# Attention in a decoder trunk on one core: the softmax steps drawn together, two residual tiles loaded a block sooner, and the maximum's tile in a pool of its own

## The chip, the cores and the metric

One core of a Trainium2 chip runs the whole program. The metric is the device time of one execution in microseconds (us). The kernel before has a median of 2106.7 us over three runs (2106.67 to 2110.82).

## What is computed

Two layers over a sequence of 1024 tokens of width 1024, all in fp32: a gated short convolution and then dilated attention, each followed by a SwiGLU network. The change touches the attention alone. Cut to that part, the reference is

```python
BRANCHES = ((128, 1), (512, 4), (2048, 16))          # window, dilation; 16 heads of 64

def dilated_attention_mixer(h, w_qkv, w_out, rel_bias):
    qkv = (h @ w_qkv).reshape(bsz, seq, 3, N_HEADS, HEAD_DIM)
    q, k, v = qkv[:, :, 0], qkv[:, :, 1], qkv[:, :, 2]
    for window, dilation in BRANCHES:
        o, l = dilated_branch(q, k, v, rel_bias, window, dilation)   # banded, causal, biased
        outs.append(o); lses.append(l)
    alpha = jax.nn.softmax(jnp.stack(lses, axis=0), axis=0)
    o = jnp.sum(alpha[..., None] * jnp.stack(outs, axis=0), axis=0)
    return o.reshape(bsz, seq, D_MODEL).astype(h.dtype) @ w_out      # added to x
```

Weighting the branches by their log-denominators is the same as one softmax over the keys of all three, and that is how the kernel computes it: for each head one maximum, one set of exponentials and one sum.

## The kernel before, in words

Every product is split: an operand becomes a rounded high part and a remainder, and three matmuls (high by high, high by low, low by high) stand for one. The two dense networks use Strassen-like schemes; they surround the attention and are not touched. The five engines each work through an instruction list of their own in order; the order in which the program's text issues the work is the order on each engine, and semaphores alone join them.

`attention` handles the 16 heads in 17 calls of `slot`, called **blocks 0 to 16** here. Block `n` holds the scores of head `n`, the softmax of head `n-1`, and the product with the values (called pv) of head `n-1`, and fills the rest of TensorE's time with dense work: up to block 10 the value projection (`value_tiles`), from block 11 on the first half of the output projection (`out_product`), whose results are added to the residual tiles `X`. A block has two halves. In the first, a loop of eight rounds takes one softmax step of the former head, one score step of this head and some dense matmuls in each round; in the second, the pv matmuls run with more dense work.

A score step gives one PSUM bank, which VectorE (DVE) empties with the bias added: into `lf` (two steps), `lh`, then `ld` and `lp` (four steps, called j0, j2, j4 and j6). Between them DVE builds the running maximum `m`: after `lh` its second half begins, after j2 its first half is complete, after j6 the second. GpSimd (POOL) then takes the maximum over the partitions of each half (`partition_all_reduce`, tile `mb`). There are eight PSUM banks, handed out in rotation.

A softmax step is a subtraction of `mb` on DVE and an exponential on ScalarE (ACT) of the same tile. There are seven: first-half `lf`, `ld`, `lp`, then second-half `lf`, `lh`, `ld`, `lp`. The pv matmuls read them in this order: first half `lf`, `ld`, `lp`; second half `lf`, `lh`, `ld`, `lp`. From block 14 on (`n > LAG`) the order is another: the softmax of a head runs whole, inside the block of its scores, and the table of this change is not read there (block 13 still reads it for head 12).

ACT also makes `kca`, a copy of the next head's keys sorted by residue, in two pieces (`classes`, in the second half of a block); the next block's first score matmuls read it.

All large tiles share one pool of 41 pages of 512 KB (`page`), used in rotation: a new tile waits until the last reader of the page's former tile is done. SyncE (SP) issues nearly all loads, in order, and an issue that waits holds up those behind it. In a block it issues the keys (`ka`), in even blocks the values (`vx`), then the queries (`qa`, `ql`) and the bias of the next head, then `oin` in blocks 9 and 10 (finished heads, read back from DRAM), then what the dense work asks for: raw weights, and in `out_product` the residual tiles `X[k]` from `spill[k]`, three tiles ahead of the one that is added to.

Of the kernel before, what the change touches and what calls it, by code (L numbers as in the profile page):

```python
# [10 lines left out]
F32 = mybir.dt.float32  # L11
# [6 lines left out]
S = 1024  # L18
# [30 lines left out]
AO_WIDE = 5  # L49
AO = 4  # L50
LAG = 13
EXTRA = (3, 7)
FILL = (("v", 0), ("v", 1), ("v", 2), ("v", 3))
OIN = LAG - 3
DENSE = (11,) * 9 + (10, 10) + (11, 11, 14, 10, 10, 9)
# [47 lines left out]
def trunk(ctx: ExitStack, tc: tile.TileContext, x, gains_in, cwi, ck, cwo, wqkv, wo, relb,  # L103
          wg, wu, wd, oneh, ident, out):
    nc = tc.nc
# [6 lines left out]
    def page(name, dt=F32):  # L112
        return pages.tile([128, 1024], dt, name=name, tag="page", bufs=PAGES)

    scope = {}
# [4 lines left out]
    def bank():  # L120
        return psum.tile([128, 512], F32, name="bank", tag="bank")
# [288 lines left out]
    X = [None] * KT  # L410
# [140 lines left out]
    class Strassen:  # L551
# [216 lines left out]
        def load_x(self, *ns):  # L768
            for n in ns:
                X[n] = page("x")  # L770
                nc.sync.dma_start(X[n], self.source[n])
# [651 lines left out]
    spill = [dram.tile([128, 1024], F32, name=f"spill{n}") for n in range(KT)]  # L1423
# [70 lines left out]
    def attention(norm, qk):  # L1494
# [57 lines left out]
        def load_kq(n):  # L1552
# [7 lines left out]
            nc.sync.dma_start(KS[n][n1].bitcast(F32), rows(k, 128 + 64 * a))  # L1560
            if n <= LAG + 1 and n % 2 == 0 and n:
                load_values(p - 1)
# [11 lines left out]
        def scores(p, a, st):  # L1574

            n = 2 * p + a
            ks, kc, qs = KS[n], KC[n], QS[n]
            q2 = qlo[a]
            bias = st["bias"]
            lf, lh, ld, lp = page("lf"), half_page("lh"), page("ld"), page("lp")  # L1580
            st.update(lf=lf, lh=lh, ld=ld, lp=lp)

            klass = lambda u: kc[:, u * 128:u * 128 + 128]
            block = lambda u: ks[:, u * 128:u * 128 + 128]

            def mm(o, k, qoff, qdims):
                nc.tensor.matmul(o, k, view(qs, qoff, qdims), start=True, stop=False)  # L1587
                nc.tensor.matmul(o, k, view(q2, qoff, qdims), start=False, stop=True)  # L1588

            kd = [[128, 4], [1, 32]]  # L1590

            for c in range(2):
                b = bank()
                for i in range(2):
                    r4 = 2 * c + i
                    mm(b[:, 256 * i:256 * i + 256], klass(r4), r4 * 32, [[512, 2], [128, 4], [1, 32]])
                for ih in range(2):
                    nc.vector.tensor_tensor(out=view(lf, ih * HALF + 64 * c, [[128, 4], [32, 2], [1, 32]]),
                                            in0=view(b, 128 * ih, [[32, 4], [256, 2], [1, 32]]),
                                            in1=view(bias, L1 + L2 - 1 - 32 * ih, [[-A2, 4], [0, 2], [-1, 32]]),  # L1600
                                            op=ALU.add)
                yield

            b = bank()
            for r4 in range(4):
                mm(b[:, 128 * r4:128 * r4 + 128], klass(4 + r4), HALF + r4 * 32, kd)
            nc.vector.tensor_tensor(out=view(lh, 0, [[128, 4], [32, 4], [1, 32]]),
                                    in0=view(b, 0, [[32, 4], [128, 4], [1, 32]]),
                                    in1=view(bias, L1 + L2 - 1, [[-A2, 4], [0, 4], [-1, 32]]), op=ALU.add)
            m = page("m")  # L1610
            st["m"] = m
            nc.vector.tensor_tensor(out=m[:, HALF:], in0=lf[:, HALF:], in1=lh, op=ALU.max)
            yield

            for j in range(0, 8, 2):
                b = bank()
                for i in range(2):
                    jj = j + i
                    if jj < 7:
                        mm(b[:, 256 * i:256 * i + 256], block(jj),  # L1620
                           blk(jj), [[blk(jj + 1) - blk(jj), 2], [32, 16], [1, 8]])
                    else:
                        mm(b[:, 256:384], block(jj), blk(jj), [[32, 16], [1, 8]])
                nc.vector.tensor_tensor(out=view(ld, blk(j), [[32, 16], [8, 2], [1, 8]]),
                                        in0=view(b, 0, [[8, 16], [256, 2], [1, 8]]),
                                        in1=view(bias, L1 - 1, [[-A1, 16], [0, 2], [-1, 8]]), op=ALU.add)
                n = 2 if j < 6 else 1
                step = blk(j + 2) - blk(j + 1) if n == 2 else 8
                nc.vector.tensor_tensor(out=view(lp, blk(j + 1), [[32, 16], [step, n], [1, 8]]),
                                        in0=view(b, 128, [[8, 16], [256, n], [1, 8]]),  # L1630
                                        in1=view(bias, L1 - 1 - 8, [[-A1, 16], [0, n], [-1, 8]]), op=ALU.add)
                if j == 2:
                    nc.vector.tensor_tensor(out=m[:, :HALF], in0=lf[:, :HALF], in1=ld[:, :HALF], op=ALU.max)
                    q = lambda t: view(t, 8, [[32, 16], [1, 24]])
                    nc.vector.tensor_tensor(out=q(m), in0=q(m), in1=q(lp), op=ALU.max)
                    mb = page("mb")
                    st["mb"] = mb
                    nc.gpsimd.partition_all_reduce(mb[:, :HALF], m[:, :HALF], 128, bass_isa.ReduceOp.max)
                yield
            nc.vector.tensor_tensor(out=m[:, HALF:], in0=m[:, HALF:], in1=ld[:, HALF:], op=ALU.max)  # L1640
            nc.vector.tensor_tensor(out=m[:, HALF:], in0=m[:, HALF:], in1=lp[:, HALF:], op=ALU.max)
            nc.gpsimd.partition_all_reduce(mb[:, HALF:], m[:, HALF:], 128, bass_isa.ReduceOp.max)
            yield
# [84 lines left out]
        put_off, ending, due = [], [], [iter(())]  # L1728
        OZ, acts = {}, {}

        def slot(n, dense, ndense, late=0, hook=iter(()), ps=()):
# [12 lines left out]
            if n + 1 < H:  # L1744
                load_kq(n + 1)
                bias[n + 1] = load_bias(n + 1)
            done.update(load_attended(ps))
            if n:
                q, b = divmod(n - 1, 2)
                if b == 0:  # L1750
                    OZ[q] = page("o"), page("z")
                old = live.pop(n - 1)
                old.update(o=OZ[q][0], z=OZ[q][1])
                pv = values(q, b, old)
            else:
                pv = iter(())
            extra = later = iter(())
            lagged = n <= LAG
            if n + 1 < H:
# [3 lines left out]
            used = 0  # L1763
            if lagged:
                for i in range(8):
                    next(due[0], None)
                    next(sc, None)
                    k = 1 + (i in EXTRA and n < LAG) if n else i % 2
                    other(k)
                    used += k  # L1770
                    if a and ending and i == 4:
                        run(ending.pop())
                run(sc)
            else:
                if a == 0 and not late:
                    other(1)
                    used += 1
                for i in range(8):
                    next(sc, None)
                    next(pv, None)  # L1780
                    next(pv, None)
                    if i >= late and i % 2 == 0:
                        other(1)
                        used += 1
                run(sc)
                run(pv)
                if a == 0:
                    extra = finish(p - 1)
                if a == 0 and n < H:
                    load_values(p)  # L1790
            left = max(ndense - used, 0)
            for i in range(8):
                next(pv, None)
                next(pv, None)
                if i == (2 if n > LAG + 1 else 5):
                    attended()
# [12 lines left out]
            run(pv)  # L1809
            run(extra)  # L1810

        def load_attended(ps):
            raw = {p: page("oin") for p in ps}
            for p in ps:
                nc.sync.dma_start(raw[p], odram[p])
            return raw
# [6 lines left out]
        def out_product(g, ps, acts):  # L1823
            for n in range(KT):
                w = take(("ao", g, n))
                for k in range(n, min(n + 3, KT)):
                    if X[k] is None:
                        X[k] = page("x")
                        nc.sync.dma_start(X[k], spill[k])
                for c in HALVES:  # L1830
                    b = bank()
                    yield from product(w, ps, acts, {c: b})
                    add_to_x(n, {c: b})
# [97 lines left out]
        sw.feed_forward(*rest, after)  # L1931
        qk.mix()
    with tc.tile_pool(name="second", bufs=1) as scope["pool"]:
        scope["halves"] = 8
        acts = attention(norm, qk)
    with tc.tile_pool(name="third", bufs=1) as scope["pool"]:
        scope["halves"] = 20
# [118 lines left out]
```

## Time and profile before

| | |
|---|---|
| median of three runs | 2106.7 us (2106.67 to 2110.82) |
| the profiled execution | 2106.85 us, of which 2105.1 us from the first to the last instruction |
| TensorE, DVE, ACT, POOL busy | 99%, 84%, 48%, 12% of the span |
| attention, blocks 0 to 15 | about 1143 to 1411 us of the span |
| scores of head 10 begin (block 10) | 1297.28 us |
| scores of head 11 begin (block 11) | 1313.27 us |
| scores of head 12 begin (block 12) | 1334.74 us |

A row of the timeline gives the start from the span's begin, the duration, the engine, the line, the operation, what is written and read, and in brackets how long the engine had been idle and what ended that. Consecutive like instructions are merged (x8). Matmul ends are modelled, and a row of matmuls may run into the next, so the rate of TensorE is read from the starts. An fp32 matmul of pv is recorded as two. A row of the stretches (windows) gives the busy time of each engine, the granted TensorE clock as a share of full speed, and the mean busy share of the 16 DMA engines.

### The profile page before, as it was taken

To read this page: it belongs to the slowest core of one execution; us is meant where nothing else is said; L and a number is where in the kernel's file an instruction comes from. 1 tells how busy PE (TensorE), PEld (TensorE's weight loads), DVE (VectorE), ACT (ScalarE), POOL (GpSimd) and SP (SyncE) were. 2 spreads that over 40 slices of the span, in tenths; PEclk is the share of its full clock that TensorE was granted. 3 is DMA by queue.
4 is the path that set the end of the run, shared out by engine and by line. 5 is a ranking of instruction groups with operands and counts; after the bars stand their busy time and mean duration, and the time that the engine had idled before them with its cause. 6 is when DMAs were issued, how large, how long until landed. Compare 5 with 4: busy or idle time off the path is not lost.

```text
span 2105.1 us, 30800 instructions
## 1 busy us (share of the span) xinstructions
PE 2080.8 (99%) x10978; PEld 1790.0 (85%) x10978; DVE 1760.2 (84%) x3308; ACT 1020.9 (48%) x1892; POOL 250.1 (12%) x352
## 2 busy tenths in 40 slices
PE   9999999999999999999999999999999999999998
PEld 7888888888888888887789999898788888888887
DVE  8898769988888888968975888887998888888886
ACT  7433427443434554445543666565644434456433
POOL 1000000110101010010323333211011001001000
PEclk9999999999999999999999999999999999999999
DMA  7322643223333466341757767855223333358432
GB/s 220 95 95 71 230 136 75 106 101 110 113 102 106 152 205 205 125 158 68 235 175 219 193 177 202 237 179 157 71 86 107 108 99 113 110 193 245 159 95 81
DMA packets 124729, 300.72 MB, mean 143 GB/s; under 512 B 15084, under 2 KB 37694, under 8 KB 124576
## 3 DMA queue, kind: packets, MB, share of 16 engines
q1 hardware_dynamic: 90720, 201.94, 31.6%
q0 software_dynamic: 26224, 82.11, 12.5%
q10 hardware_dynamic: 7632, 14.70, 1.9%
q8 instruction: 87, 1.43, 0.3%
q14 instruction: 66, 0.54, 0.1%
HBM read 208.42 MB, written 82.93 MB: 138 GB/s over the span
## 4 chain that ended last, share of the span: by engine, by line
PE 48%; DVE 4%; ACT 1%; DMA 1%; issue 0%; DVEq 0%; ACTq 0%
PE bank L587 9%; PE bank L585 9%; PE bank L586 9%; PE bank L1662 4%; PE bank L387 2%; PE bank L389 2%; PE bank L388 2%; PE bank L1531 1%; PE bank L677 1%; PE bank L1533 1%; PE bank L1532 1%; PE bank L680 1%; PE bank L679 1%; PE bank L1588 1%; PE bank L1587 1%; DVE w L147 1%
## 5 line engine op out<-in xcount | busy, mean ns | idle before, releaser
L587 PE MATMUL bank<-b,w 128*128 128x512 f32 x2008 | 782.6, 390 | 4.8 <-DVE w L147 4.5
L585 PE MATMUL bank<-b,w 128*128 128x512 f32 x2008 | 782.7, 390 | 4.4 <-ACT w L146 2.2
L586 PE MATMUL bank<-b,w 128*128 128x512 f32 x2008 | 782.1, 390 | 0.6 <-DVE b L896 0.6
L587 PEld LDWEIGHTS bank<-b,w 128*128 128x128 f32 x2008 | 376.9, 188 | 88.1 <-DVE w L147 9.9
L585 PEld LDWEIGHTS bank<-b,w 128*128 128x128 f32 x2008 | 377.2, 188 | 82.7 <-ACT w L146 3.3
L586 PEld LDWEIGHTS bank<-b,w 128*128 128x128 f32 x2008 | 377.2, 188 | 78.1 <-DVE b L896 1.2
L146 ACT ACTIVATE w<-combo 128x512 fp32r<-128x512 f32 (+2 forms) x496 | 253.9, 542 | 239.2 <-DVE combo L207 220.4
L147 DVE TENSOR_TENSOR w<-combo,w 128x512 fp32r<-128x512 f32 (+2 forms) x496 | 282.6, 583 | 37.8 <-ACT w L146 37.0
L591 ACT ACTIVATE part<-bank 128x512 f32<-128x512 f32 x192 | 114.2, 595 | 381.0 <-PE bank L587 379.1
L147 DVE TENSOR_TENSOR w<-raw,w 128x512 fp32r<-128x512 f32 (+2 forms) x348 | 193.1, 576 | 38.9 <-ACT w L146 38.9
L595 DVE TENSOR_TENSOR part<-part,bank 128x256 f32<-128x256 f32 (+1 forms) x372 | 175.2, 501 | 32.0 <-PE bank L587 17.4
L146 ACT ACTIVATE w<-raw 128x512 fp32r<-128x512 f32 (+2 forms) x348 | 170.5, 531 | 56.1 <-PE bank L587 21.5
L387 PE MATMUL bank<-w_hi,w 128*128 128x512 f32 (+1 forms) x400 | 151.8, 380 | 0.1
L389 PE MATMUL bank<-w_hi,w 128*128 128x512 f32 (+1 forms) x400 | 149.5, 374 | 0.7 <-DVE w L147 0.7
L388 PE MATMUL bank<-w_lo,w 128*128 128x512 f32 (+1 forms) x400 | 149.3, 373 | 0.0
L506 DVE TENSOR_TENSOR x<-x,bank 128x512 f32<-128x512 f32 (+1 forms) x104 | 66.6, 644 | 63.4 <-PE bank L389 58.2
L815 DVE TENSOR_TENSOR x<-x,bank 128x512 f32<-128x512 f32 x136 | 92.9, 683 | 28.6 <-PE bank L587 28.6
L207 DVE TENSOR_TENSOR combo<-raw 128x512 f32<-128x512 f32 (+1 forms) x176 | 114.0, 649 | 0.0
L389 PEld LDWEIGHTS bank<-w_hi,w 128*128 128x128 f32 x400 | 75.5, 189 | 15.1 <-DVE w L147 1.6
L578 DVE TENSOR_TENSOR b<-hin,b 128x512 fp32r<-128x512 f32 x126 | 79.6, 686 | 9.3 <-ACT b L577 9.2
L387 PEld LDWEIGHTS bank<-w_hi,w 128*128 128x128 f32 x400 | 75.7, 189 | 11.9 <-ACT w L146 0.5
L388 PEld LDWEIGHTS bank<-w_lo,w 128*128 128x128 f32 x400 | 75.8, 189 | 11.6
(228 smaller groups left out, 3352.1 us busy)
## 6 DMA issues: line engine op xcount, KB each, us to landing
hin<-part SPq DMA_DIRECT2D x126, 256.0 KB, 5.0
raw<-in_ffn_w_gate SPq DMA_DIRECT2D x44, 512.0 KB
raw<-in_ffn_w_up SPq DMA_DIRECT2D x44, 512.0 KB, 3.7
part<-sum POOLq DMA_DIRECT2D x72, 256.0 KB, 2.3
raw<-in_ffn_w_down SPq DMA_DIRECT2D x48, 384.0 KB, 3.2
raw<-in_attn_w_qkv SPq DMA_DIRECT2D x27, 512.0 KB, 5.3
raw<-in_conv_w_in SPq DMA_DIRECT2D x24, 512.0 KB, 3.6
part<-part POOLq DMA_DIRECT2D x36, 256.0 KB, 2.5
```

The costliest lines, as they stand in the source:

```text
L146: nc.scalar.activation(hi, src, AF.Copy)
L147: low = lambda: eng.tensor_tensor(out=lo, in0=src, in1=hi, op=ALU.subtract)
L207: eng.tensor_tensor(out=c, in0=a, in1=b, op=op)
L387: nc.tensor.matmul(b, whi[:, a], ahi[:, s], start=first, stop=False)
L388: nc.tensor.matmul(b, whi[:, a], alo[:, s], start=False, stop=False)
L389: nc.tensor.matmul(b, wlo[:, a], ahi[:, s], start=False, stop=last)
L585: nc.tensor.matmul(b, hi[:, a], bhi, start=start and k == 0, stop=False, skip_group_check=True)
L586: nc.tensor.matmul(b, hi[:, a], blo, start=False, stop=False, skip_group_check=True)
L587: nc.tensor.matmul(b, lo[:, a], bhi, start=False, stop=k == n - 1, skip_group_check=True)
L591: nc.scalar.activation(t, b, AF.Copy)
L595: nc.vector.tensor_tensor(out=t, in0=t, in1=b, op=ALU.add)
L815: nc.vector.tensor_tensor(out=X[n][:, half(h)], in0=X[n][:, half(h)], in1=b, op=ALU.add)
```

## The change

Four edits.

1. A table `PIECES` says how many softmax steps each of the eight rounds takes: 1, 1, 2, 2, 1 and then none, where it was one in each of the first seven.
2. At the start of block 10 (`n == OIN`), behind the loads of `oin`, the residual tiles `X[0]` and `X[1]` are loaded. `out_product` no longer finds them missing in block 11 and loads `X[2]` there.
3. The tile `m` comes from a pool of two buffers of its own, tagged `max`, and no longer from the 41 pages.
4. The pool of half pages in the attention has 4 buffers and not 8, which is the room that the two buffers of `m` take.

```diff
+PIECES = (1, 1, 2, 2, 1) + (0,) * 3
...
-            m = page("m")
+            m = scope["pool"].tile([128, S], F32, name="m", tag="max", bufs=2)
...
             done.update(load_attended(ps))
+            if n == OIN:
+                for k in range(2):
+                    load_x(k)
...
             if lagged:
                 for i in range(8):
-                    next(due[0], None)
+                    for _ in range(PIECES[i]):
+                        next(due[0], None)
                     next(sc, None)
...
+        def load_x(k):
+            if X[k] is None:
+                X[k] = page("x")
+                nc.sync.dma_start(X[k], spill[k])
...
                 for k in range(n, min(n + 3, KT)):
-                    if X[k] is None:
-                        X[k] = page("x")
-                        nc.sync.dma_start(X[k], spill[k])
+                    load_x(k)
...
     with tc.tile_pool(name="second", bufs=1) as scope["pool"]:
-        scope["halves"] = 8
+        scope["halves"] = 4
```

TensorE's list is the same, instruction for instruction. In the changed kernel line numbers are higher by one from here on, and by more behind `load_x`.

DVE in block 11, from the `lh` score step to the second residual add. A row whose source and target is `mb` and one of `lf`, `lh`, `ld`, `lp` is a softmax subtraction, `x<-x,bank` is the residual add. Before:

```order
L1607 TENSOR_TENSOR lh<-bank,bias 128x512
L1612 TENSOR_TENSOR m<-lf,lh 128x512
L1651 TENSOR_TENSOR lf<-lf,mb 128x512
L1624 TENSOR_TENSOR ld<-bank,bias 128x16x16
L1629 TENSOR_TENSOR lp<-bank,bias 128x16x16
L1651 TENSOR_TENSOR lh<-lh,mb 128x512
L1624 TENSOR_TENSOR ld<-bank,bias 128x16x16
L1629 TENSOR_TENSOR lp<-bank,bias 128x16x2x8
L1633 TENSOR_TENSOR m<-lf,ld 128x512
L1635 TENSOR_TENSOR m<-m,lp 128x16x24
L506 TENSOR_TENSOR x<-x,bank 128x512
L1651 TENSOR_TENSOR ld<-ld,mb 128x512
```

The same place on DVE after the change, from the same `lh` score step on; the row just ahead of it is now `lf<-lf,mb`:

```order
L1608 TENSOR_TENSOR lh<-bank,bias 128x512
L1613 TENSOR_TENSOR m<-lf,lh 128x512
L1652 TENSOR_TENSOR lh<-lh,mb 128x512
L1652 TENSOR_TENSOR ld<-ld,mb 128x512
L1625 TENSOR_TENSOR ld<-bank,bias 128x16x16
L1630 TENSOR_TENSOR lp<-bank,bias 128x16x16
L1652 TENSOR_TENSOR lp<-lp,mb 128x512
L1625 TENSOR_TENSOR ld<-bank,bias 128x16x16
L1630 TENSOR_TENSOR lp<-bank,bias 128x16x2x8
L1634 TENSOR_TENSOR m<-lf,ld 128x512
L1636 TENSOR_TENSOR m<-m,lp 128x16x24
L507 TENSOR_TENSOR x<-x,bank 128x512
```

The four second-half subtractions moved up: `lf` ahead of the `lh` score step, `lh` and `ld` ahead of j0, `lp` ahead of j2. All stand ahead of the residual add now, where `ld` and `lp` stood behind it. The same move is made in blocks 1 to 13.

SP at the end of the loads of block 10, into block 11 (`odram` holds finished heads, `kq` keys and queries, `vdram` values). Before:

```order
L1815 DMA oin<-odram_88 128x1024
L170 DMA raw<-in_attn_w_out 128x512
L1559 DMA ka<-kq_1_2926 64x1024
L1560 DMA ka<-kq_1_2926 64x1024
L1546 DMA vx<-vdram_95 128x8x128
L1549 DMA vx<-vdram_95 128x4x128 x2
L1564 DMA qa<-kq_0_2925 64x1024 x2
L1565 DMA ql_10353<-kq_0_2925 64x1024
L1482 DMA bias<-tables 128x1x361
L1483 DMA bias<-tables 128x1x349
L1829 DMA x<-spill_77 128x1024
L1829 DMA x<-spill_78 128x1024
```

The same place on SP after the change:

```order
L1825 DMA oin<-odram_88 128x1024
L1820 DMA x<-spill_77 128x1024
L1820 DMA x<-spill_78 128x1024
L171 DMA raw<-in_attn_w_out 128x512
L1560 DMA ka<-kq_1_2926 64x1024
L1561 DMA ka<-kq_1_2926 64x1024
L1547 DMA vx<-vdram_95 128x8x128
L1550 DMA vx<-vdram_95 128x4x128 x2
L1565 DMA qa<-kq_0_2925 64x1024 x2
```

The two residual loads moved past eleven issues: one of raw weights, two of keys, three of values, three of queries and two of the bias.

## Prediction, before the run

> **What bounds the kernel now.** I read the page's busy shares first, then the waits of TensorE over the attention (1130 to 1500 us), then the timelines of the engines that those waits name, then 4-us stretches around them.
>
> ```profile
> span 2105.1 us, 30800 instructions
> PE 2080.8 (99%) x10978; PEld 1790.0 (85%) x10978; DVE 1760.2 (84%) x3308; ACT 1020.9 (48%) x1892; POOL 250.1 (12%) x352
> ...
> PE bank L1662 <- ACT ld L1652: 2.0, 1, 2.0
> PE bank L1662 <- ACT lp L1652: 1.0, 2, 0.8
> ```
>
> TensorE is busy for 2080.8 of 2105.1 us and its instruction list does not change. So the change can only give back time in which TensorE stands idle or runs at a lower clock, at most 24.3 us plus what the clock costs, and it can only lose time by making TensorE wait where it does not wait now. In the waits, pv (L1662) waits three times for an exponential: once for `ld`, 2.0 us, and twice for `lp`, 1.0 us. Where these are, TensorE's timeline shows (blocks 6, 9, 10 and 11, the ends of pv and the starts of the next scores):
>
> ```profile
> 1246.43 0.39 PE L1662 MATMUL bank<-ld,vx 128*128 128x128 f32 x2
> 1247.08 0.49 PE L1662 MATMUL bank<-lp,vx 128*128 128x128 f32 x2 [0.27 <-ACT lp L1652]
> ...
> 1297.13 0.39 PE L1662 MATMUL bank<-lp,vx 128*128 128x128 f32 x2
> 1297.28 0.37 PE L1587 MATMUL bank<-qa,kca 128*128 128x256 f32 x1
> ...
> 1310.15 1.06 PE L1662 MATMUL bank<-lh,vx 128*128 128x128 f32 x8
> 1311.04 0.39 PE L1662 MATMUL bank<-ld,vx 128*128 128x128 f32 x2
> 1311.28 0.49 PE L1662 MATMUL bank<-lp,vx 128*128 128x128 f32 x2
> ...
> 1312.72 0.39 PE L1662 MATMUL bank<-lp,vx 128*128 128x128 f32 x2
> 1313.27 0.38 PE L1587 MATMUL bank<-qa,kca 128*128 128x256 f32 x1 [0.16 <-ACT kca L1571]
> ...
> 1323.71 1.05 PE L1662 MATMUL bank<-lf,vx 128*128 128x128 f32 x8
> 1327.06 1.06 PE L1662 MATMUL bank<-lh,vx 128*128 128x128 f32 x8
> 1330.11 0.49 PE L1662 MATMUL bank<-ld,vx 128*128 128x128 f32 x2 [2.00 <-ACT ld L1652]
> 1331.38 0.49 PE L1662 MATMUL bank<-lp,vx 128*128 128x128 f32 x2 [0.78 <-ACT lp L1652]
> ```
>
> The two large waits are both in block 11. DVE's timeline, block 10 above and block 11 below, says why:
>
> ```profile
> 1306.58 0.42 DVE L1624 TENSOR_TENSOR ld<-bank,bias 128x256 f32<-128x256 f32 x1
> 1307.24 0.68 DVE L1633 TENSOR_TENSOR m<-lf,ld 128x512 f32<-128x512 f32 x1
> 1308.44 0.68 DVE L1651 TENSOR_TENSOR ld<-ld,mb 128x512 f32<-128x512 f32 x1
> 1309.04 0.42 DVE L1624 TENSOR_TENSOR ld<-bank,bias 128x256 f32<-128x256 f32 x1
> 1309.71 0.86 DVE L1651 TENSOR_TENSOR lp<-lp,mb 128x512 f32<-128x512 f32 x1
> ...
> 1318.72 0.68 DVE L1607 TENSOR_TENSOR lh<-bank,bias 128x512 f32<-128x512 f32 x1
> 1320.06 0.68 DVE L1651 TENSOR_TENSOR lf<-lf,mb 128x512 f32<-128x512 f32 x1
> 1320.66 0.42 DVE L1624 TENSOR_TENSOR ld<-bank,bias 128x256 f32<-128x256 f32 x1
> 1323.30 0.56 DVE L1635 TENSOR_TENSOR m<-m,lp 128x384 f32<-128x384 f32 x1
> 1328.10 0.69 DVE L506 TENSOR_TENSOR x<-x,bank 128x512 f32<-128x512 f32 x1 [4.25 <-DMA x<-spill]
> 1328.71 0.68 DVE L1651 TENSOR_TENSOR ld<-ld,mb 128x512 f32<-128x512 f32 x1
> ```
>
> In block 11 DVE reaches the first residual add, finds `X[0]` not landed, and stands for 4.25 us. The second half's `ld` and `lp` subtractions are queued behind that add. Their exponentials follow, and pv behind those. In block 10, without a residual add, the same `ld` subtraction runs at 1308.44.
>
> ```profile
> 1310.60 0.63 ACT L1652 ACTIVATE lp<-lp 128x512 f32<-128x512 f32 x1 [0.81 <-DVE lp L1651]
> 1312.08 1.13 ACT L1571 ACTIVATE kca<-ka 128x512 fp32r<-128x512 f32 x1
> ...
> 1308.00:1312.00 4.00, 4.00 (x37) 3.96 (x36) 3.96 (x9) 2.03 (x3) 2.14 (x1) 1.00 0.87 257
> 1312.00:1316.00 4.00, 3.80 (x28) 3.12 (x27) 2.97 (x6) 3.96 (x6) 2.15 (x1) 1.00 0.39 104
> 1332.00:1336.00 4.00, 4.00 (x19) 3.64 (x19) 4.00 (x6) 3.95 (x6) 2.35 (x2) 0.57 1.02 224
> ...
> 1298.35 7.64 SPq L1815 DMA_DIRECT2D oin<-odram  x2
> 1307.09 0.59 SPq L1560 DMA_DIRECT2D ka<-kq  x1
> 1313.14 0.38 SPq L1546 DMA_DIRECT2D vx<-vdram  x1
> 1318.81 3.43 SPq L1829 DMA_DIRECT2D x<-spill  x3
> ```
>
> These are ACT, the stretches (PE, PEld, DVE, ACT, POOL busy, then clock, DMA share, GB/s) and SP's queue. Behind the two waits the granted clock is 0.57 over 1332 to 1336, where it is 1.00 before. `X[0]` is issued only at 1318.81.
>
> **The change part by part.**
>
> *Steps drawn together, and the early loads.* They act on the same stall, so I price them as one. With the table, block 11's four second-half subtractions stand ahead of the add. Before, `ld` would have had to wait for it; now it is issued ahead of the j0 adds, that is at about 1320.66 plus the two moved subtractions of 0.60 us (start to start, 1320.06 to 1320.66), some 1321.9, and not 1328.71. pv wants it near 1327.06 + 0.89 = 1327.95, by the 0.89 us that block 10 takes from `lh` to `ld` (1310.15 to 1311.04). Even with the exponential of 0.63 us behind it, it is over 5 us early. So the table alone takes this stall away, and so would the loads alone: `X[0]`, issued behind `oin`, at about 1298.35 + 7.64 = 1306.0, would be in place well before 1323.9. What they give back:
>
> - `ld`: (1330.11 − 1327.06) − 0.89 = 2.16 us.
> - `lp`: (1331.38 − 1330.11) − (1311.28 − 1311.04) = 1.27 − 0.24 = 1.03 us.
> - The clock: 4.00 × (1 − 0.57) = 1.72 us of TensorE's work in the stretch behind. It is the only drop in this part and lies right behind the two waits, so I count it as theirs.
>
> On the clock, the Trainium skill's page "TensorE: Matmul & The Clock Gate", Part 1, says that the array falls to half after an idle window of some 3.4 us. The waits here are 2.00 and 0.78 us with a short burst between them, together less than that. Read strictly, the rule would not tie the drop to this stall, and the sum would lack the 1.72 us; that is rival B.
>
> *The table in the other blocks.* In block 10 `lp`'s subtraction moves from behind the j4 adds to ahead of the j2 adds. It passes the j2 pair (1306.58 to 1307.24, 0.66), the two maximum operations (1307.24 to 1308.44, 1.20) and the j4 pair (1309.04 to 1309.71, 0.67), so it ends 2.5 us sooner. Its exponential now ends at 1310.60 + 0.63 = 1311.23 and its matmul starts at 1311.28: no margin before, 2.5 us after. Two small waits of this kind go:
>
> - block 6: (1247.08 − 1246.43) − 0.24 = 0.41 us on `lp`.
> - block 11's first scores wait for ACT's `kca` copy, which starts at 1312.08 behind the late `lp`: (1313.27 − 1312.72) − (1297.28 − 1297.13) = 0.55 − 0.15 = 0.40 us.
>
> What pays on DVE: the `lh` adds come 0.6 us later, j0 and j2 1.2 us, j4 0.6, j6 nothing; the work is only put in another order. A later add frees its bank later, and TensorE is the one that would wait. In block 11 the `lh` add ends at 1318.72 + 0.68 = 1319.40 and pv takes over a bank of that turn at 1323.71, so 0.6 us comes out of 4.3 us: nothing on the path. On ACT the copies now stand behind exponentials that come earlier, and ACT is at 48%. Bounds for this edit beyond the two waits: a gain of 0.9 us more, if small excesses of a few tenths in other blocks go as well (about as much again as the two above), and a loss by the last rival's price. I take zero, since no row shows either.
>
> *`X[0]` and `X[1]` ahead on SP.* The two issues (3.43/3 = 1.1 us each) now stand ahead of eleven others: a raw weight, the keys, the values, queries and bias of the next block. The values (`vx`) are issued at 1313.14, 5.5 us after the queue's last issue (1307.09 + 0.59), so 2.3 us of issuing vanish in that gap. The bytes do not: 2 × 512 KB at the 257 GB/s of 1308 to 1312 are 4.1 us of the DMA engines. In 1312 to 1316 these are 39% busy, which leaves 2.4 us free, and 1308 to 1312 leaves 0.5 more. So `vx` may land up to 4.1 − 2.9 = 1.2 us later. pv needs it at 1323.71, ten microseconds after its issue. I take zero; the bound is rival A.
>
> *`m` in its own pool, four half pages.* The page rotation shifts by one tile a block. No wait is seen for either; zero, covered by the gap between a tile's last reader and its next use. If it isn't covered, it is a load's delay as in rival A.
>
> *The sum:* 2.16 + 1.03 + 1.72 + 0.40 + 0.41 = 5.72 us. The profiled execution took 2106.85 us, 0.15 us over the median of 2106.7, so I take the sum from 2106.85: **2101.1 us**.
>
> **A second rule.** These rows are DVE's and POOL's where a subtraction fell beside the first reduction:
>
> ```profile
> 1243.57 1.53 DVE L1651 TENSOR_TENSOR ld<-ld,mb 128x512 f32<-128x512 f32 x1
> ...
> 1242.69 2.61 POOL L1638 PARTITION_ALL_REDUCE mb<-m  x1 [10.32 <-issue]
> ```
>
> The subtraction took 1.53 us and not 0.68, the reduction 2.61. That subtraction now comes ahead of the reduction; what falls beside it instead are j4 and j6 adds, which read a bank, and the maximum operations behind them. By these rows the exposure is at most 0.85 us of DVE in a block, before or after, inside 2.5 us of new margin; I count nothing. The Trainium skill, "SBUF — State Buffer", under Terms, calls the port that the two engines share an exclusive lock on which the loser fully blocks; by that, an operation that meets the whole reduction could lose up to its 2.6 us once in a block, which speaks against any order that puts two-input operations there. The two stretched rows agree with a lock in kind, and their size is less.
>
> **The rivals.**
>
> A. *The loads hold up the next block.* `vx` lands late by up to 1.2 us, behind 1 MB in a queue that is 87% busy at 1308 to 1312. For it: block 10's own loads took 7.64 us to issue. Against it: `vx` has ten microseconds. Where pv then waits up to 1.6 us (the 1.2 and an issue's 0.4), it gives 2101.1 + 1.6 = 2102.7, and with a clock drop behind it 2104.4.
>
> B. *The clock drop is not the wait's.* Then 1.72 us stays: 2102.8. Against it: the drop starts right behind the waits.
>
> C. *No gain.* The stall goes, another takes its place: in block 12 the DMA engines are at 1.02 of their time in 1332 to 1336, and TensorE, arriving 5 us sooner, then waits for queries or weights that land when they did. Or the reordering isn't effective, because the subtraction's data or its bank are late. 2105 to 2107.
>
> D. *Slower: the banks.* The `lh` adds come 0.6 us and the j0 and j2 adds 1.2 us later in 13 blocks. If DVE already runs behind in a block by more than 4.3 − 0.6 = 3.7 us, by reductions that stretch its work as above and by its other work (it is 84% busy), every delay passes to TensorE: 13 × 0.6 = 7.8 to 13 × 1.2 = 15.6 us, on 2101.1 this is 2108.9 to 2116.7. It comes out slower from 0.76 us in a block on (2110.9, 0.2% over the median, less 2101.1, over 13). For it: DVE has full stretches (3.96 of 4.00). Against it: no wait of TensorE in the attention names a bank held by an add.
>
> **How the numbers follow.** The forecast with its own small bounds (2101.1 less 0.9 and 0.3 of run-to-run scatter; more by 1.3, half of the clock term and the two small waits' half) is 2099.9 to 2102.4; I give it 0.67. A and B together 0.14, C 0.06, D 0.13. The range takes in A and B: 2099.9 to 2104.4, which leaves out C and D, 0.19. A difference of 0.2%, 4.2 us, is about what a measurement of this kernel can tell from no change. Faster by more than that means below 2102.5: the forecast and a part of A (0.03), 0.70. Within it lie B, the rest of A, C and the lower part of D, 0.19. Slower is the upper part of D, 0.11.
>
> **What would show it.** In the profile after, block 11's `ld` and `lp` subtractions stand ahead of a residual add that waits for nothing; pv's rows of block 11 follow at 0.89 and 0.24 us; the clock is 1.00 through 1320 to 1340; `kca` and `lp` are gone from TensorE's waits. Wrong would be: a wait of pv for `vx` in block 11 (A); a clock below 1 without a gap ahead of it (B); a gap at block 12's first scores or weights (C); waits of score or pv matmuls for DVE's adds, recurring in blocks 1 to 13 (D).

## The result

| | before | changed |
|---|---|---|
| median of ten runs each | 2109.14 us (2105.44 to 2110.82) | 2102.11 us (2100.34 to 2104.01) |
| profiled execution | 2106.85 us | 2101.97 us |

The ratio is 0.9970, 95% interval [0.9961, 0.9980]; a second measurement gave 0.9975 [0.9963, 0.9986]. The kernel became 0.25 to 0.3% faster. The two profiled executions differ by 4.88 us.

On the page of the changed kernel the span is 2100.2 us (2105.1 before), and TensorE is busy for 2079.6 us of it (2080.8). TensorE's waits in blocks 0 to 15 of the attention (1143 to 1411 us):

```profile
PE bank L1588 <- ACT kca L1572: 0.8, 1, 0.8
```

The three waits of pv are gone, and one has come that the profile of before does not have at this place: 0.8 us for `kca`. Block 11 on TensorE, and DVE with the subtractions ahead of the residual add:

```profile
1327.04 1.06 PE L1663 MATMUL bank<-lh,vx 128*128 128x128 f32 x8
1327.94 0.39 PE L1663 MATMUL bank<-ld,vx 128*128 128x128 f32 x2
1328.16 0.39 PE L1663 MATMUL bank<-lp,vx 128*128 128x128 f32 x2
...
1319.68 0.68 DVE L1608 TENSOR_TENSOR lh<-bank,bias 128x512 f32<-128x512 f32 x1
1321.61 0.68 DVE L1652 TENSOR_TENSOR ld<-ld,mb 128x512 f32<-128x512 f32 x1
1322.88 0.68 DVE L1652 TENSOR_TENSOR lp<-lp,mb 128x512 f32<-128x512 f32 x1
1325.34 0.68 DVE L507 TENSOR_TENSOR x<-x,bank 128x512 f32<-128x512 f32 x1
```

And the stretches behind (their length, the busy time of PE, PEld, DVE, ACT and POOL, the clock, the DMA share, GB/s):

```profile
1328.00:1332.00 4.00, 4.00 (x31) 3.73 (x31) 4.00 (x6) 2.07 (x5) 2.35 (x2) 1.00 1.06 255
1332.00:1336.00 4.00, 4.00 (x26) 3.53 (x25) 3.97 (x9) 2.41 (x4) 0.00 (x0) 1.00 1.04 257
```

From `lh` to `ld` pv now takes 0.90 us and from `ld` to `lp` 0.22 us. The `ld` subtraction starts at 1321.61, not 1328.71; the residual add waits for nothing; the clock is 1.00 in both stretches.

The new wait lies in block 10. TensorE's row, then ACT's rows ahead of it:

```profile
1299.81 0.33 PE L1588 MATMUL bank<-qa,kca 128*128 128x128 f32 x1 [0.84 <-ACT kca L1572]
...
1294.87 1.06 ACT L147 ACTIVATE w_hi<-oin 128x1024 fp32r<-128x1024 f32 x1 [3.25 <-DMA oin<-odram]
1295.84 1.15 ACT L1572 ACTIVATE kca<-ka 128x512 fp32r<-128x512 f32 x1
1297.68 1.06 ACT L147 ACTIVATE w_hi<-oin 128x1024 fp32r<-128x1024 f32 x1 [0.70 <-DMA oin<-odram]
1298.65 1.11 ACT L1572 ACTIVATE kca<-ka 128x512 fp32r<-128x512 f32 x1
```

The second `kca` copy stands on ACT behind the split of an `oin` tile (the row `w_hi<-oin`). ACT waits for that tile's DMA, and the copy is late.

### The profile page after: what moved, and what is told of

Same layout as the page of the kernel before. It is cut to its first block, busy times and chain, and to the rows that moved or that the text cites. A ratio compares the mean times of both kernels' runs of the same rounds, so it can differ in the third digit from the quotient of the medians.

```text
span 2100.2 us, 30796 instructions
## 1 busy us (share of the span) xinstructions
PE 2079.6 (99%) x10978; PEld 1790.1 (85%) x10978; DVE 1757.9 (84%) x3308; ACT 1023.0 (49%) x1892; POOL 247.4 (12%) x352
## 4 chain that ended last, share of the span: by engine, by line
PE 49%; DVE 2%; ACT 1%; DMA 0%; issue 0%; SPq 0%; DVEq 0%; ACTq 0%
PE bank L588 9%; PE bank L586 9%; PE bank L587 9%; PE bank L1663 4%; PE bank L388 2%; PE bank L390 2%; PE bank L389 2%; PE bank L1532 1%; PE bank L678 1%; PE bank L1534 1%; PE bank L1533 1%; PE bank L681 1%; PE bank L680 1%; PE bank L1589 1%; PE bank L1588 1%; DMA oin<-odram 0%
```

## The experiments

My theory: block 11's stall was softmax work standing on DVE behind an add that waited for a late tile, so that either the table or the early loads alone takes it away. The rivals are those of the prediction.

**The table alone**, on the kernel before:

```
+PIECES = (1, 1, 2, 2, 1) + (0,) * 3
-                    next(due[0], None)
+                    for _ in range(PIECES[i]):
+                        next(due[0], None)
```

> The kernel before with the table of steps alone; X[0] is issued where it was. Theory (the stall is the second half's ld and lp subtractions standing behind the residual add): both stand ahead of it now, so pv of block 11 waits for nothing although DVE still waits some 3 us for X[0]. Gain as for the whole change, 5 to 7 us (about 2102). Rival (the late residual tile itself is the cause): DVE's wait then holds the j4 and j6 adds and the second maximum, TensorE stops a little later, and less than half of the gain is left (2106 or more).

Measured 2101.79 us; ratio 0.9974 [0.9964, 0.9984]. DVE, and pv on TensorE:

```profile
1320.74 0.68 DVE L1652 TENSOR_TENSOR ld<-ld,mb 128x512 f32<-128x512 f32 x1
1322.00 0.68 DVE L1652 TENSOR_TENSOR lp<-lp,mb 128x512 f32<-128x512 f32 x1
1327.22 0.69 DVE L507 TENSOR_TENSOR x<-x,bank 128x512 f32<-128x512 f32 x1 [2.68 <-DMA x<-spill]
...
1326.17 1.06 PE L1663 MATMUL bank<-lh,vx 128*128 128x128 f32 x8
1327.06 0.39 PE L1663 MATMUL bank<-ld,vx 128*128 128x128 f32 x2
```

`X[0]` is late here and DVE waits 2.68 us for it. TensorE does not notice, because nothing that it wants soon stands behind that add. The late tile by itself was not the cause; what stood behind it was.

**The early loads alone**, on the kernel before (cut; `load_x` is as in the change):

```
+            if n == OIN:
+                for k in range(2):
+                    load_x(k)
```

> The kernel before with X[0] and X[1] loaded in block 10 alone; one softmax step a round as before. Theory: the residual add waits for nothing, so the subtractions behind it are on time and pv of block 11 waits for nothing. The two small waits on late lp (block 6, 0.4 us, and kca in block 11, 0.4 us) stay. Gain 4 to 6 us. Rival (the order on DVE is the cause): less than half of the gain. Rival A of the prediction: a wait of pv for vx of up to 1.6 us.

Measured 2103.84 us; ratio 0.9980 [0.9972, 0.9989]. Block 11 on DVE (the subtraction again behind the add), and TensorE's waits in the attention:

```profile
1324.81 0.68 DVE L506 TENSOR_TENSOR x<-x,bank 128x512 f32<-128x512 f32 x1
1325.41 1.25 DVE L1651 TENSOR_TENSOR ld<-ld,mb 128x512 f32<-128x512 f32 x1
```

The waits:

```profile
PE bank L1587 <- ACT kca L1571: 0.3, 1, 0.3
PE bank L1662 <- ACT lp L1652: 0.3, 1, 0.3
```

The add waits for nothing, and pv of block 11 neither. Block 6's wait for `lp` stays, as expected. The other small wait that was to stay, block 11's for `kca`, is not there: the 0.3 us of `kca` in the list lie in block 10 (1300.47 us). There is no wait for `vx`. On block 11's stall the two parts do the same thing twice. The intervals of the two ratios overlap, but they share their baseline: seven of the nine runs of the table lie under the lowest of the eleven with the loads (2102.42 us), and the medians are 2.05 us apart. Here the table is the better one. Block 6's wait accounts for some 0.4 us of that; the rest was not traced.

**The rooms alone** (`m` in its own pool, four half pages), on the kernel before:

> The kernel before with the maximum's tile in its own pool and four half pages alone. Theory: no change, within 0.1% (2 us). Rival: the 41 pages were what made block 11's loads late, and the time falls by 1 us or more, with X[0] issued earlier than 1318.8 us.

Measured 2107.41 us; ratio 0.9998 [0.9990, 1.0007]: no difference is seen, and `X[0]` is issued at 1320.21, not earlier. The stall and the slow clock are there in this profile too (waits of TensorE, then the stretch behind). The wait for `kca` lies in block 10, and block 11's is missing here too:

```profile
PE bank L1662 <- ACT ld L1652: 1.4, 1, 1.4
PE bank L1662 <- ACT lp L1652: 1.0, 2, 0.8
PE bank L1587 <- ACT kca L1571: 0.3, 1, 0.3
```

The stretch:

```profile
1332.00:1336.00 4.00, 4.00 (x20) 3.87 (x21) 3.96 (x6) 3.95 (x6) 2.35 (x2) 0.62 1.03 217
```

**A late exponential, ten copies**, on the changed kernel. It asks how much margin pv has and what a wait does to the clock, without a DMA in it (cut; the remarks are added here):

```
+                if dst is last:                      # the second half of ld, in block 11
+                    for _ in range(more):            # 10, or 16
+                        nc.scalar.activation(dst, dst, AF.Copy)
                 nc.scalar.activation(dst, dst, AF.Exp)
```

> The changed kernel with ten extra copies of half of ld onto itself on ACT ahead of that half's exponential, in block 11 alone (about 0.55 to 0.6 us each, 5.5 to 6 us). In the changed kernel the exponential could end some 5 us later before pv wants it. Theory: pv waits once, 0.5 to 1.2 us for ld and under 0.5 us for lp, and the clock stays at 1.00 behind it. Rival B (a clock drop comes with the stall's place and not its length): a stretch at half clock follows all the same, or none ever follows.

ACT's copies, pv's wait and the stretch behind it:

```profile
1322.75 6.61 ACT L1656 ACTIVATE ld<-ld 128x512 f32<-128x512 f32 x10
...
1330.07 0.49 PE L1667 MATMUL bank<-ld,vx 128*128 128x128 f32 x2 [1.55 <-ACT ld L1657]
```

The stretch behind:

```profile
1332.00:1336.00 4.00, 4.00 (x26) 3.27 (x25) 4.00 (x9) 3.94 (x7) 0.57 (x1) 1.00 1.06 207
```

The copies took 6.61 us, more than I reckoned, so the wait was 1.55 us and not up to 1.2; the `lp` matmul behind it did not wait. The margin is 6.61 − 1.55 = 5.06 us, as expected. The clock stayed at 1.00. One execution took 2104.95 us.

**A late exponential, sixteen copies:**

> The same with sixteen copies (8.8 to 9.6 us). Theory: pv waits 3.8 to 4.6 us for ld and about 0.4 us for lp, TensorE's clock falls to half for 3.4 us behind that, and all that follows is later by the wait and 1.7 us. Rival B: the wait without a drop, as the drop of the kernel before wasn't the wait's.

```profile
1324.36 10.56 ACT L1656 ACTIVATE ld<-ld 128x512 f32<-128x512 f32 x16
...
1335.64 0.80 PE L1667 MATMUL bank<-ld,vx 128*128 128x128 f32 x2 [5.50 <-ACT ld L1657]
```

The stretches (the wait, and what is behind it):

```profile
1332.00:1336.00 4.00, 0.36 (x1) 0.36 (x2) 0.00 (x0) 3.84 (x7) 0.44 (x1) 0.66 1.03 255
1336.00:1340.00 4.00, 4.00 (x18) 3.88 (x18) 2.43 (x3) 4.00 (x6) 0.57 (x1) 0.50 1.07 211
```

The margin is the same: 10.56 − 5.50 = 5.06 us. The wait was longer than expected, again by the copies' price. The drop came, at the same place in the program, and was about twice as long as forecast: 0.34 and 0.50 of two stretches of 4 us, 3.4 us of TensorE's work (part of it, ahead of 1335.64, while it waited). One execution took 2111.62 us. The place alone brings no drop, since there was none with ten copies, and a wait without a late transfer brings one: rival B falls. That the length of the wait alone decides is not shown by one execution of each, and the section on the prediction gives rows against it.

**All steps in two rounds**, on the changed kernel: `PIECES = (4, 3) + (0,) * 6`.

> The changed kernel with the table (4, 3, 0, ...): all seven softmax steps within the first two rounds, so the lh adds of 13 blocks come some 2.4 us later than in the kernel before, four times what the change does to them. Theory: a bank is wanted again some 4 us after the add, so TensorE waits nowhere, and the time is the changed kernel's within 1.5 us. Rival D (a later add passes to TensorE in every block): 13 x 0.6 us or more on top, 2110 or more, and waits of score or pv matmuls for DVE's adds in blocks 1 to 13.

Measured 2103.26 us; ratio 0.9977 [0.9968, 0.9987], not told apart from the changed kernel. TensorE's waits in the attention, and the `lh` add of block 11:

```profile
PE bank L1588 <- ACT kca L1572: 0.4, 1, 0.4
```

The add:

```profile
1320.36 0.68 DVE L1608 TENSOR_TENSOR lh<-bank,bias 128x512 f32<-128x512 f32 x1
```

The add is 1.64 us later than in the kernel before (1318.72) and not 2.4: DVE stood idle for 1.03 us ahead of its first `lf` add of block 11 there (1314.05), and some of the steps now fill that time. Still, it is over twice the 0.6 us of the prediction, and no matmul waits for a bank. Rival D has no foothold.

**Four residual tiles early**, on the changed kernel: `range(4)` for `range(2)`.

> The changed kernel with four residual tiles loaded at the start of block 10 and not two: 1 MB more ahead of vx. Theory: the changed kernel's vx landed about 3 us before pv of block 11 needs it, two more tiles are 2.6 to 4.1 us of the DMA engines at 404 to 257 GB/s, so pv waits 0 to 1.5 us for vx at 1323.7. Rival A in full strength: vx lands 4 us or more late and pv waits over 1.5 us, with a clock drop; rival to both: the transfers share the engines and vx is not later at all.

TensorE waits for nothing in the attention. A row of TensorE from the start of the program, SP's rows, and pv's first matmuls of block 11:

```profile
60.03 0.79 PE L588 MATMUL bank<-b,w 128*128 128x512 f32 x1 [2.13 <-DVE w L148]
...
1308.40 2.06 SPq L1820 DMA_DIRECT2D x<-spill  x4
1315.54 0.38 SPq L1547 DMA_DIRECT2D vx<-vdram  x1
...
1325.54 1.05 PE L1663 MATMUL bank<-lf,vx 128*128 128x128 f32 x8
```

Twice the early load cost pv nothing: there is no bracket on its first row, so it did not wait. Whether `vx` landed later, these rows don't say. All of this lies 1.8 us later in the span than in the changed kernel (1325.54 for 1323.70), without a wait in the attention. The time was lost at the start of the program: TensorE waited 2.13 us for a weight and not 0.93 us as in the changed kernel (shown below), and the clock was 0.59 over 60 to 64 us. One execution took 2103.91 us. Rival A falls at this load; at which load it would begin wasn't tried.

**The copies ahead of the splits**, on the changed kernel (the remark is added here):

```
-                if i < 4:
+                if i < 4 if n != OIN - 1 else i > 2:
                     next(hook, None)                 # a split of oin
```

> The changed kernel, with one thing more: in block 9 ACT makes the two kca copies ahead of the two splits of oin, which wait for their DMA. Theory: the new wait of 0.84 us for kca at 1299.8 us in the changed kernel goes, and nothing else moves: 0.8 us under the changed kernel, about 2101.3. Rival: the wait was a chance of one execution, or the splits come too late for block 11 and cost as much: no gain.

Measured 2101.15 us (2100.47 to 2101.27); ratio 0.9968 [0.9956, 0.9981]. TensorE's waits in the attention: none. ACT:

```profile
1291.92 2.20 ACT L1572 ACTIVATE kca<-ka 128x512 fp32r<-128x512 f32 x2
...
1297.88 1.06 ACT L147 ACTIVATE w_hi<-oin 128x1024 fp32r<-128x1024 f32 x1 [1.18 <-DMA oin<-odram]
```

ACT still waits for `oin`, but nothing stands behind it. The trace shows the wait gone; the 0.96 us between the medians is less than the intervals resolve.

**The changed kernel again:**

> The changed kernel once more, unaltered, beside the next one: 2101 to 2104, no wait of pv in block 11 and no clock drop there. Whether the wait of 0.84 us for kca in block 10 is there again tells if it was a chance of one execution: theory (the split of oin stands ahead of kca on ACT and waits for its DMA) has it again, at 0.2 to 0.9 us; the other reading has none.

Measured 2101.76 us. The `kca` wait of block 10 is there again:

```profile
PE bank L1588 <- ACT kca L1572: 0.9, 2, 0.5
```

It was 0.2 us with the table alone and 0.3 us with the loads or the rooms alone, where the profile of before has none in that block. With four early tiles, whose program is the changed kernel's up to block 10, there is none either. So it is not the work of one part of the change; why the copy is late in one execution and in time in another stays open.

**The table and the copies alone**, without early loads and rooms:

> The kernel before with the table of steps and with the two kca copies of block 9 ahead of the splits of oin, without the early residual tiles and without the rooms. Theory: the table alone is what the change is worth and the copies take the last wait in blocks 9 to 11, so 0 to 1 us under the changed kernel, about 2101.2. Rival: the early tiles are worth something when the rest is out of the way, and it is slower than the changed kernel.

Measured 2100.86 us (2100.33 to 2103.74); ratio 0.9971 [0.9960, 0.9983], and no wait of TensorE in the attention. That is no slower than the whole change (2101.76 beside it), nor than the whole change with the same copies (2101.15, measured earlier). The early tiles show no worth of their own.

## Why the prediction was right, and where it was not

**Size and baseline.** Forecast 2101.1 us, measured 2102.11, within the range. That it came so near is in part luck. The execution that I took as the base (2106.85) lay 2.29 us under the median of ten, and the gain between medians was 7.03 us where 5.72 was summed; the two errors offset each other but for 1 us. In the second measurement the gain was 6.24 us. Further medians of the kernel before were 2107.95 (25 runs), 2107.97 and 2108.00 us. What makes up the gain between medians beyond the rows below was not traced.

**Block 11, 3.19 us.** From the rows, (3.05 − 0.90) + (1.27 − 0.22) = 3.20 us. That table and loads are each enough was forecast and is shown by each alone.

**The clock, 1.72 us.** It went with the stall. Eight profiles without that wait (the changed kernel twice among them) show no drop in block 11, and the two with it do (the kernel before and the rooms alone). What I left out is that the base had a piece of luck elsewhere. The start of the program, TensorE's waits and the stretch behind them, in the kernel before:

```profile
25.28 0.50 PE L585 MATMUL bank<-b,w 128*128 128x512 f32 x1 [1.59 <-ACT w L146]
26.68 0.50 PE L587 MATMUL bank<-b,w 128*128 128x512 f32 x1 [0.67 <-DVE w L147]
58.84 0.50 PE L587 MATMUL bank<-b,w 128*128 128x512 f32 x1 [1.25 <-DVE w L147]
```

The stretch:

```profile
28.00:32.00 4.00, 4.00 (x19) 3.33 (x18) 3.93 (x7) 4.00 (x8) 1.00 (x2) 1.00 0.08 14
```

The same in the changed kernel:

```profile
24.78 0.50 PE L586 MATMUL bank<-b,w 128*128 128x512 f32 x1 [1.75 <-ACT w L147]
26.18 0.50 PE L588 MATMUL bank<-b,w 128*128 128x512 f32 x1 [0.67 <-DVE w L148]
58.99 0.50 PE L588 MATMUL bank<-b,w 128*128 128x512 f32 x1 [0.93 <-DVE w L148]
```

The stretch:

```profile
28.00:32.00 4.00, 4.00 (x13) 3.12 (x12) 3.93 (x7) 4.00 (x8) 1.50 (x2) 0.67 0.17 33
```

Nearly the same waits brought half clock in one execution and not in the other, and their length does not sort them: 1.55 + 0.67 us brought 0.58 over 28 to 32 us with the copies ahead of the splits, 1.60 + 0.68 us left 1.00 with the ten copies. Where a wait falls does more. In one execution all drops begin whole steps of 3.4133 us apart: with the rooms alone at 27.71, 1331.60 and 2099.60 us, and 1303.89 / 382 and 768.00 / 225 both give 3.4133. In the kernel before they begin at 1332.58 and 2100.58 us, again 225 steps apart. The two steps around block 11's drop there, the one ahead of it and the drop itself:

```profile
1329.17:1332.58 3.41, 1.69 (x12) 1.50 (x13) 3.38 (x9) 2.52 (x4) 0.00 (x0) 1.00 1.06 293
1332.58:1335.99 3.41, 3.41 (x14) 3.06 (x13) 3.41 (x5) 3.36 (x6) 2.35 (x2) 0.50 1.03 229
```

The second wait and about half of the first fell into one step, and TensorE was busy for 1.69 us of its 3.41. The wait of 1.55 us with ten copies fell almost whole into one step, which stayed busier (1.97 us) as nothing else was missing in it:

```profile
1326.55:1329.96 3.41, 1.97 (x18) 1.78 (x16) 2.96 (x7) 3.25 (x7) 2.17 (x2) 1.00 1.05 331
1329.96:1333.38 3.42, 3.27 (x21) 2.63 (x22) 1.86 (x3) 3.42 (x6) 1.20 (x2) 1.00 1.05 237
```

So it seems that a step in which TensorE is busy for about half of the time or less brings the drop in the next one. The border is not sharp in these rows (1.81 us busy with a drop in the copies ahead of the splits, 1.55 us without one in the table and copies, both at the start), the ends of matmuls are modelled, and no run sets where a wait falls. Whether a stall like block 11's costs the 1.72 us in every execution is open.

In the pair above the drop cost little, since DVE was late at 59 us anyway: the changed kernel is only 0.15 us behind there. But the base was early at that row. In ten of the other eleven profiles it comes later than 58.84, by 0.15 to 1.19 us. With four early tiles the start alone cost over 1.8 us more. This is a source of the scatter between runs; how much of it was not measured.

**The small waits.** Block 6's `lp` and block 11's `kca` went, 0.81 us, as summed. Block 11's is not the table's for certain: it was missing with the loads alone and the rooms alone too, where TensorE reached those scores about 1 us later in the span. With the table and the copies alone it is gone, and there no wait in block 10 stands ahead of it. The step that failed is "On ACT the copies now stand behind exponentials that come earlier, and ACT is at 48%", which put the cost on ACT at nothing: the share of ACT said nothing about a copy behind a split that waits for a DMA. That order was there before the change, with hardly any margin. Block 10's second copy on ACT and the matmul that reads it, in the kernel before:

```profile
1297.67 1.12 ACT L1571 ACTIVATE kca<-ka 128x512 fp32r<-128x512 f32 x1
...
1299.03 0.22 PE L1587 MATMUL bank<-qa,kca 128*128 128x128 f32 x1
```

The copy ended at 1298.79, 0.24 us ahead of that matmul. In the changed kernel it ended at 1299.76, and the new wait took 0.84 us back. The balance of the two profiles closes with it: 5.72 − 0.84 = 4.88 us, the measured difference; what else differs is a few tenths, which cancel.

**No cost on DVE's adds, none for vx, none for the rooms.** All three were taken as zero, and the runs that pushed each (steps in two rounds, four tiles, rooms alone) agree.

## What to carry to other kernels

When an engine stands on a late transfer, look at what is queued behind that instruction and who wants it. Moving the wanted work ahead of the wait was worth at least as much here as making the transfer early, cost nothing that the runs show, and left the engine waiting 2.68 us for nobody. Then look for the same pattern on the next engine: a copy behind a split that waited for a DMA took back 0.84 us until it, too, was moved ahead. And before a sum is set against one profiled execution, compare that execution with several medians.

## What the hardware showed that I had not expected

- The half clock does not need one long wait: 1.4 and 0.8 us with a short burst between them brought it (the rooms alone), and 1.55 + 0.67 us at the start brought 0.58 where 1.60 + 0.68 us left the clock at 1.00. Single waits do not sort by length either: behind one of 1.80 us at 59.49 us (sixteen copies) the clock was 0.57 over 60 to 64 us, behind one of 1.87 us at 59.54 us (the table and the copies) it was 1.00. The Trainium skill, "TensorE: Matmul & The Clock Gate", Part 1, says that the activity window of 3.4 us is free-running, which would make such cases depend on where the window lies. The traces agree: drops of one execution begin whole steps of 3.4133 us apart. The rows don't fit the same page's abstract rule, "no PE-idle gaps >~3.4µs" (under "HAM oscillation — how this bites in real kernels"), if it is read to mean that shorter gaps are harmless.
- The first maximum over partitions of block 10 took 2.14 us on POOL with a subtraction (`ld`, 1308.44 for 0.68 us) running as it began, and 1.78 us once the subtractions stood ahead. A maximum operation of two tiles that fell into the second half of the shorter one (1310.55) did not stretch it. In block 6, where the prediction reads 2.61 us beside a subtraction, the reduction took 2.68 us in the changed kernel (1243.98) with no subtraction beside it; in both a split's remainder (`w_lo<-raw,w_hi`) was running as it began. So the subtraction was not needed to make that one long. The two rows of block 10:

```profile
1308.62 2.14 POOL L1638 PARTITION_ALL_REDUCE mb<-m  x1 [10.80 <-DVE m L1635]
...
1309.61 1.78 POOL L1639 PARTITION_ALL_REDUCE mb<-m  x1 [12.28 <-DVE m L1636]
```
